# Modulation passes of a two-layer encoder trunk: pinned to other places in four stages, with their buffers kept to the end and 2 KB of scratch for dynamic transfers

## The chip, the cores and the metric

The kernel runs on one core of one Trainium2 chip. The metric is the time of one execution on the device in microseconds (us); the runs shown are of the kernel before, three times, and one execution that was taken with the hardware profiler. TensorE is called PE, VectorE DVE, ScalarE ACT, GpSimd POOL, and SP is the engine whose queue issues nearly all transfers here.

## The reference, cut to what matters

One sequence of 512 tokens with 1024 features goes through two layers. Every norm is followed by a shift and a scale, and every residual add by a gate, and these vectors come from one conditioning vector `c`. The modulation is what the change is about:

```python
c_act = jax.nn.silu(c)
mod = c_act @ mod_w[layer] + mod_b[layer]                  # two layers, 6 vectors of 1024 each
sh1, sc1, g1, sh2, sc2, g2 = jnp.split(mod, N_MOD, axis=-1)
u = modulate(rms_norm(h, norm_mix[layer]), sh1, sc1)       # x * (1 + scale) + shift
mix = hgrn2_mixer(u, ...)  # layer 0;  chunk_band_attention(u, k_pad, v_pad, ...)  in layer 1
h = h + g1 * mix
u = modulate(rms_norm(h, norm_ffn[layer]), sh2, sc2)
h = h + g2 * swiglu(u, ffn_w_in[layer], ffn_w_out[layer])
# after layer 0 a shared K/V of the same h, with its own shift and scale (shk, sck)
```

So there are 14 modulation vectors, each 1024 long, each the product of a 1024 x 1024 matrix with one vector.

## The kernel before, in words

**Layout and stages.** The residual stream `h` lies in SBUF as 8 tiles of 128 features x 512 tokens. All weights stream from HBM in blocks of 512 KB, in the order of `weight_plan`, each split by ACT (line 123 or 496) and DVE (line 128 or 497) into a high and a low part, so that a product is three matmuls (lines 183 to 185). The stages in order of time are: start and first projections; the mixer of layer 0 (`core`, lines 712 to 852, four pairs of heads, whose DVE steps at lines 732 and 733 each must end before PE's next small products at line 757); its output projection `ao`; the first FFN; shared K/V and attention (lines 1109 to 1291); the second FFN.

**An FFN** (`ffn`, `fast_tiles`) has four plain hidden tiles, then 18 tiles of a Strassen-like scheme with 7 half-size products each (lines 531 to 533), for which DVE builds sums of weight blocks (`f_x`, lines 510 to 515) and their low parts (`f_w_l`, line 497), and then the output projection `f_o` in chunks. Both FFNs run the same code; only the first of them carries modulation work in the kernel before.

**A modulation pass.** A vector is computed on DVE, not on PE: for each of its 8 blocks of 128 outputs a row block of the matrix (128 x 1024, 512 KB, tile `mw`) is loaded by SP at line 313, and one DVE instruction at line 315 multiplies it with `crow` (the activated `c` in every partition) and adds up along the row; a second, short instruction (`DVE_READ_ACCUMULATOR`) writes the sum out. Eight passes make one vector (line 317). The first two vectors are done at the start in another way; the other twelve are 96 passes. Two buffers of tag `mraw` hold the rows, so a load waits until the pass before the last has been read.

**What sets the order.** `mod_vectors` is a Python generator, `side`; each `next(side)` emits one load and one pass. Before, six vectors were emitted in the mixer and the `ao` stage (48 passes: in `push` from position 50 of the filler on, at every 7th and later every 3rd position; then in `ao`, with the rest at n = 5), and six in the first FFN (48 passes: after every second fast tile, and after the output chunks). The emitted program then goes through a list scheduler that puts each engine's instructions in an order by a model of its own. `tc.issue_after(state["mods_after"].ins)` keeps a pass from standing ahead of the named instruction; in the kernel before, `mods_after` is set once near the start of the mixer (line 1028) and once for each input of a fast FFN (line 352), so that the scheduler is free to place the passes anywhere after those. Each engine executes its own order strictly, and SP issues its loads strictly in order, weights and `mw` rows in one queue.

**Memory.** The buffers of the passes (`mods`: `crow` and two `mraw`) are closed after the first FFN (line 1103). 16 KB of every partition are the default scratch for transfers that POOL issues; there are four of these (line 126), two in each FFN.

## Time and profile before

| what | value |
|---|---|
| median of 3 runs | 1267.31 us (1263.37 to 1268.36) |
| the profiled execution's own time | 1264.94 us |
| its span in the profile | 1263.2 us |
| granted TensorE clock, mean | 0.995 |
| PE busy | 1238.8 us (98%) |
| DVE busy | 986.2 us (78%) |
| ACT busy | 644.6 us (51%) |
| passes: busy time of line 315 | 116.8 us in 96, mean 1220 ns |

Shares of the page are averages over stages; the views by stretch (windows) give busy time of each engine between two moments. PE's matmuls are pipelined, so that a busy PE need not be at its peak; equal work that takes longer in one stage than in another shows the difference.

### The profile page before, as it was taken

The numbers are of one execution on the slowest core, as the hardware profiler recorded it, in microseconds if no ns is written. First come the engines' busy times: TensorE is split into PE (matmuls) and PEld (weight loads), VectorE is DVE, ScalarE is ACT, GpSimd is POOL, SyncE is SP. The second block draws the span as 40 slices with busy tenths as digits, with TensorE's granted clock in tenths as the row PEclk, the third lists the DMA queues.
The fourth block names the chain that finished last, engine by engine and source line by source line (L and its number), as shares of the span: only waits on it lengthen the run. The fifth ranks groups of instructions, "written<-read, shape, count | busy, mean of one in ns | idle before, by whom it ended". The sixth has DMA issues, their size and how long they took to land.

```text
span 1263.2 us, 21610 instructions
## 1 busy us (share of the span) xinstructions
PE 1238.8 (98%) x8560; PEld 1072.5 (85%) x8560; DVE 986.2 (78%) x1805; ACT 644.6 (51%) x1132; POOL 21.9 (2%) x29
## 2 busy tenths in 40 slices
PE   7999999999999999999999999999999999999997
PEld 6888778788899999978888877777889999998887
DVE  7998988947899999987357867776798888884323
ACT  4464446353645555653227656675465556574221
POOL 0000000000000000000000000000000000000000
PEclk8999999999999999999999999999999999999999
DMA  9455666613265555567333332221342332342331
GB/s 362 178 184 185 219 232 218 201 67 101 78 223 175 190 185 185 186 215 244 93 101 110 109 94 87 74 68 35 115 117 92 111 116 102 101 126 92 92 92 67
DMA packets 52533, 177.55 MB, mean 141 GB/s; under 512 B 5968, under 2 KB 8400, under 8 KB 52432
## 3 DMA queue, kind: packets, MB, share of 16 engines
q1 hardware_dynamic: 51856, 174.08, 41.2%
q0 software_dynamic: 576, 2.10, 1.0%
q8 instruction: 67, 1.10, 0.4%
q14 instruction: 34, 0.28, 0.1%
HBM read 171.96 MB, written 2.10 MB: 138 GB/s over the span
## 4 chain that ended last, share of the span: by engine, by line
PE 74%; DVE 12%; DMA 6%; ACT 4%; issue 3%; POOL 1%; SPq 0%; DVEq 0%; POOLq 0%; ACTq 0%
PE f_r L532 8%; PE f_r L533 7%; PE f_r L531 7%; PE f_o L185 6%; PE f_o L183 6%; PE f_o L184 6%; DVE mw L315 3%; DMA mw<-in_modw 2%; DMA r_f_c<-in_ffn_in 2%; DVE f_w_l L497 1%; PE ao L183 1%; PE ao L185 1%; PE ao L184 1%; PE av L206 1%; PE bo L183 1%
## 5 line engine op out<-in xcount | busy, mean ns | idle before, releaser
L532 PE MATMUL f_r<-f_l,f_w_h 128*128 128x256 f32 x1008 | 286.8, 285 | 0.0
L533 PE MATMUL f_r<-f_h,f_w_l 128*128 128x256 f32 x1008 | 282.1, 280 | 1.8 <-DVE f_w_l L497 1.7
L531 PE MATMUL f_r<-f_h,f_w_h 128*128 128x256 f32 x1008 | 280.8, 279 | 0.0
L533 PEld LDWEIGHTS f_r<-f_h,f_w_l 128*128 128x128 f32 x1008 | 189.0, 188 | 3.2 <-DVE f_w_l L497 3.0
L531 PEld LDWEIGHTS f_r<-f_h,f_w_h 128*128 128x128 f32 x1008 | 189.5, 188 | 0.3 <-ACT f_pu L553 0.2
L532 PEld LDWEIGHTS f_r<-f_l,f_w_h 128*128 128x128 f32 x1008 | 189.5, 188 | 0.1
L183 PE MATMUL f_o<-f_p,f_o_h 128*128 128x512 f32 (+1 forms) x374 | 142.3, 380 | 0.0
L184 PE MATMUL f_o<-f_p,f_o_h 128*128 128x512 f32 (+1 forms) x374 | 140.9, 377 | 1.0 <-DVE f_p L448 1.0
L185 PE MATMUL f_o<-f_p,f_o_l 128*128 128x512 f32 (+1 forms) x374 | 141.5, 380 | 0.2
L315 DVE SCALAR_TENSOR_TENSOR mw<-mw,crow 128x1024 f32<-128x1024 f32 x96 | 116.8, 1220 | 14.9 <-DMA mw<-in_modw 14.7
L123 ACT ACTIVATE f_o_h<-r_f_o 128x1024 fp32r<-128x1024 f32 (+1 forms) x48 | 46.8, 987 | 135.0 <-PE f_o L184 100.6
L128 DVE TENSOR_TENSOR f_o_l<-r_f_o,f_o_h 128x1024 fp32r<-128x1024 f32 (+1 forms) x48 | 54.0, 1133 | 70.6 <-ACT f_o_h L123 64.2
L496 ACT ACTIVATE f_w_h<-f_x 128x1024 fp32r<-128x1024 f32 x72 | 76.5, 1062 | 48.8 <-PE f_r L532 41.4
L497 DVE TENSOR_TENSOR f_w_l<-f_x,f_w_h 128x1024 fp32r<-128x1024 f32 x72 | 88.0, 1223 | 5.0 <-ACT f_w_h L496 2.6
L496 ACT ACTIVATE f_w_h<-r_f_c 128x1024 fp32r<-128x1024 f32 x72 | 61.0, 847 | 49.2 <-PE f_r L532 48.4
L185 PEld LDWEIGHTS f_o<-f_p,f_o_l 128*128 128x128 f32 x374 | 70.1, 188 | 16.0 <-DVE f_o_l L128 1.9
L184 PEld LDWEIGHTS f_o<-f_p,f_o_h 128*128 128x128 f32 x374 | 70.2, 188 | 15.1 <-DVE f_p L448 1.4
L183 PEld LDWEIGHTS f_o<-f_p,f_o_h 128*128 128x128 f32 x374 | 70.3, 188 | 12.5
L497 DVE TENSOR_TENSOR f_w_l<-r_f_c,f_w_h 128x1024 fp32r<-128x1024 f32 x72 | 68.8, 955 | 10.0 <-ACT f_w_h L496 10.0
L1179 ACT ACTIVATE sb<-sb,st 128x128 f32<-128x128 f32 (+1 forms) x64 | 35.7, 558 | 36.4 <-DVE st L1178 36.1
L1176 DVE CUSTOM_DVE_ANT_0 sb<-s,wb 128x128 f32<-128x128 f32 (+1 forms) x64 | 30.8, 486 | 15.0 <-PE s L1173 14.8
L185 PE MATMUL f<-f_h,f_l 128*128 128x512 f32 x96 | 37.4, 396 | 0.0
(397 smaller groups left out, 2728.1 us busy)
## 6 DMA issues: line engine op xcount, KB each, us to landing
mw<-in_modw SPq DMA_DIRECT2D x96, 512.0 KB, 4.2
r_f_c<-in_ffn_in SPq DMA_DIRECT2D x72, 512.0 KB, 3.4
r_f_o<-in_ffn_out SPq DMA_DIRECT2D x32, 512.0 KB, 3.6
mrow<-in_modw SPq DMA_DIRECT2D x16, 512.0 KB, 8.8
r_f<-in_ffn_in SPq DMA_DIRECT2D x16, 512.0 KB, 3.4
r_f_o<-in_ffn_out SPq DMA_DIRECT2D x16, 384.0 KB, 3.2
r_av<-in_a_v SPq DMA_DIRECT2D x8, 512.0 KB, 3.9
r_g<-in_a_g SPq DMA_DIRECT2D x8, 512.0 KB, 4.7
```

The costliest lines, as they stand in the source:

```text
L123: A.activation(wh, raw, AF.Copy)
L128: V.tensor_sub(wl, raw, wh)
L183: T.matmul(ps, wh[:, kt, :], uh, start=start, stop=False)
L184: T.matmul(ps, wh[:, kt, :], ul, start=False, stop=False)
L185: T.matmul(ps, wl[:, kt, :], uh, start=False, stop=stop)
L315: V.scalar_tensor_tensor(mw, mw, 1.0, crow, op0=ALU.mult, op1=ALU.mult, accum_out=raw[:, j:j + 1])
L496: A.activation(wh, raw, AF.Copy)
L497: V.tensor_sub(wl, raw, wh)
L531: T.matmul(ps, wh[:, j, :], uh, start=f, stop=False, skip_group_check=True)
L532: T.matmul(ps, wh[:, j, :], ul, start=False, stop=False, skip_group_check=True)
L533: T.matmul(ps, wl[:, j, :], uh, start=False, stop=stop and j == 3, skip_group_check=True)
L1179: A.activation(s[:, 0:n], s[:, 0:n], AF.Exp, bias=st[:, 1:2], accum_out=st[:, 2:3])
```

## The change

**How passes are emitted.** `mod_vectors` becomes one generator over all steps of the vectors that it is given. It loads its rows ahead: one row ahead with the two `mraw` buffers, or two rows ahead when it is given a second pool, in which two more buffers (`mraw2`) hold every other row. Its first `next` only loads.

**Where.** 32 passes (g1, sc2, sh2, g2) in the mixer, at every 5th position of the filler from 55 on, with four buffers, and none in `ao`; 40 in the first FFN (sck, shk, sc1b, sh1b, g1b), after two of three fast tiles, two after each chunk of the first output pair and four for each later output tile, with four buffers; 16 in attention (sc2b, sh2b), at every third unit of scores, two buffers; 8 in the second FFN (g2b), after two of three fast tiles.

**Pinned.** `mods_after` now follows the program: it is set by the low splits of the mixer's and the output projections' weights, by the second instruction of `advance` in the mixer, by the last instruction of each fast tile and by the normalising multiply of each unit of scores. A pass cannot stand earlier than the latest of these at the moment when it was emitted.

**Memory.** The scratch for POOL's transfers is 2 KB, and the `mods` pool stays open to the end of the kernel.

```diff
-            V.tensor_sub(wl, raw, wh)
+            low = V.tensor_sub(wl, raw, wh)
+            if key[0] in ("av", "g", "zf", "q", "ao") or key[1] == "o":
+                state["mods_after"] = low
...
+    def mod_vectors(names, extra=None):
+        steps = [(vectors.index(v), j) for v in names for j in range(KT)]
+        ahead = 2 if extra else 1
...
+                pool, tag = (extra, "mraw2") if extra and n % 2 else (mp, "mraw")
+                rows[n] = pool.tile([P, D], F32, tag=tag, name=f"mw{i}_{j}", bufs=2)
+                nc.sync.dma_start(out=rows[n], in_=d["modw"][i, j])
...
+        for n, (i, j) in enumerate(steps):
+            load_row(n + ahead)
...
             with tc.issue_after(state["mods_after"].ins):
                 V.scalar_tensor_tensor(mw, mw, 1.0, crow, op0=ALU.mult, op1=ALU.mult, accum_out=raw[:, j:j + 1])
...
-                    for _ in range(3):
+                    for _ in range(2):
                         next(side, None)
...
-                        for _ in range(1 + (fast and ci < 2)):
+                        for _ in range(1 + (fast and ci == 0)):
                             next(side, None)
...
-            V.tensor_mul(row2, row2, p5)
+            last = V.tensor_mul(row2, row2, p5)
             kept(n, at)
-            if i % 2:
+            if i % 3:
+                state["mods_after"] = last
                 next(side, None)
...
-            V.tensor_mul(kv, kv, t2[:, :, 1:2].to_broadcast([P, n, hh]))
+            state["mods_after"] = V.tensor_mul(kv, kv, t2[:, :, 1:2].to_broadcast([P, n, hh]))
...
-    side = mod_vectors(("g1", "sc2", "sh2", "g2", "sck", "shk"))
+    side = mod_vectors(("g1", "sc2", "sh2", "g2"), hp)
+    MODS_FROM = 55
...
-            if pos > 49 and pos % (7 if pos < 114 else 3) == 0:
+            if pos >= MODS_FROM and pos % 5 == 0:
                 next(side, None)
...
-    side = mod_vectors(("sc1b", "sh1b", "g1b", "sc2b", "sh2b", "g2b"))
...
-    ffn(0, z0, u, mod["g2"], side, finish)
-    mods.close()
+    with tc.tile_pool(name="mx", bufs=1) as mx:
+        ffn(0, z0, u, mod["g2"], mod_vectors(("sck", "shk", "sc1b", "sh1b", "g1b"), mx), finish)
...
-            V.tensor_scalar_mul(s[:, 0:n], s[:, 0:n], st[:, 3:4])
+            state["mods_after"] = V.tensor_scalar_mul(s[:, 0:n], s[:, 0:n], st[:, 3:4])
...
+        side = mod_vectors(("sc2b", "sh2b"))
...
+            if k % 3 == 2:
+                next(side, None)
...
-    ffn(1, z0, u, mod["g2b"], iter(()), finish)
+    ffn(1, z0, u, mod["g2b"], mod_vectors(("g2b",)), finish)
...
-    nc = _bacc.Bacc("TRN2", target_bir_lowering=False, num_devices=1)
+    nc = _bacc.Bacc("TRN2", target_bir_lowering=False, num_devices=1, dynamic_dma_scratch_size=2048)
```

**How it moves instructions.** Three places on DVE. The passes are the rows with `mw`; their line is 315 before and 334 in the changed kernel, and other lines are shifted likewise.

The first place is the mixer, at the start of the second pair of heads; `zf_l` and `q_l` are low parts of weights, and `qq` and `ks` the steps that PE's next small products wait for. Before:

```order
L315 SCALAR_TENSOR_TENSOR mw_4_1798,mcol_1673<-mw_4_1798,crow 128x1024
L128 TENSOR_TENSOR q_l<-r_q_1284,q_h 128x1024
L315 SCALAR_TENSOR_TENSOR mw_5_1829,mcol_1673<-mw_5_1829,crow 128x1024
L315 SCALAR_TENSOR_TENSOR mw_6_1841,mcol_1673<-mw_6_1841,crow 128x1024
L128 TENSOR_TENSOR zf_l<-r_zf_1374,zf_h 128x1024
L732 TENSOR_TENSOR qq_508<-qq_508,f_509 128x512
L733 TENSOR_TENSOR ks_906<-ks_906,f_509 128x512
```

The same place in the changed kernel:

```order
L861 TENSOR_TENSOR oe_1270<-o_1233,ors_1254 128x512
L127 TENSOR_TENSOR q_l<-r_q_1291,q_h 128x1024
L127 TENSOR_TENSOR zf_l<-r_zf_1384,zf_h 128x1024
L752 TENSOR_TENSOR qq_508<-qq_508,f_509 128x512
L753 TENSOR_TENSOR ks_906<-ks_906,f_509 128x512
```

The passes ahead of `zf_l`, `qq` and `ks` are gone from here; the next one stands six rows further down.

The second place is the first FFN, between the steps of its fast tiles 8 and 9 (`f_w_l` are the low parts that PE waits for). Before:

```order
L497 TENSOR_TENSOR f_8_w_l<-r_f_8_c_4005,f_8_w_h 128x512
L515 TENSOR_TENSOR f_9_x_4263<-r_f_9_c_4129,f_9_x_4262 128x512
L560 TENSOR_TENSOR f_pu_4195<-f_r_8_4194,f_pu_4195 128x256
L315 SCALAR_TENSOR_TENSOR mw_2_6058,mcol_5961<-mw_2_6058,crow 128x1024
L497 TENSOR_TENSOR f_9_w_l<-r_f_9_c_4129,f_9_w_h 128x1024
L567 TENSOR_TENSOR f_ar_3936<-f_qu_4196 128x256
L568 TENSOR_TENSOR f_ar_3936<-f_r_8_4193,f_pu_4195 128x256
L315 SCALAR_TENSOR_TENSOR mw_3_6061,mcol_5961<-mw_3_6061,crow 128x1024
L497 TENSOR_TENSOR f_9_w_l<-f_9_x_4262,f_9_w_h 128x1024
```

The same place in the changed kernel:

```order
L518 TENSOR_TENSOR f_8_w_l<-r_f_8_c_3956,f_8_w_h 128x512
L581 TENSOR_TENSOR f_pu_4147<-f_r_8_4146,f_pu_4147 128x256
L518 TENSOR_TENSOR f_9_w_l<-r_f_9_c_4084,f_9_w_h 128x1024
L588 TENSOR_TENSOR f_ar_3887<-f_qu_4148 128x256
L589 TENSOR_TENSOR f_ar_3887<-f_r_8_4145,f_pu_4147 128x256
L590 TENSOR_TENSOR f_ar_3887<-f_ar_3887,f_pu_4147 128x256
L518 TENSOR_TENSOR f_9_w_l<-f_9_x_4214,f_9_w_h 128x1024
L518 TENSOR_TENSOR f_9_w_l<-f_9_x_4215,f_9_w_h 128x1024
L593 TENSOR_TENSOR f_ar_3887<-f_ar_3887,f_qu_4148 128x256
L334 SCALAR_TENSOR_TENSOR mw_1_3885,mcol_4016<-mw_1_3885,crow 128x1024
```

One pass is left for this tile, and it stands behind the low parts shown; among the rows of the fast tiles as a whole ten passes are left.

The third place is attention, at the seventh pair of heads: `sb` is a unit of scores, `ta` and `tb` the query parts that PE's next scores wait for, `bo_l` a low part of a later weight. Before:

```order
L1178 TENSOR_SCALAR st_3_8612<-st_3_8612 128x1
L1180 RECIPROCAL st_3_8612<-st_3_8612 128x1
L1181 TENSOR_SCALAR sb_3_8611<-sb_3_8611,st_3_8612 128x512
L1155 SCALAR_TENSOR_TENSOR ta_8628<-bq_8558,ta_8628 64x512
L1156 SCALAR_TENSOR_TENSOR tb_8629<-bq_8558,tb_8629 64x512
L128 TENSOR_TENSOR bo_l<-r_bo_8634,bo_h 128x1024
```

The same place in the changed kernel:

```order
L1195 TENSOR_SCALAR st_3_8584<-st_3_8584 128x1
L127 TENSOR_TENSOR bo_l<-r_bo_8609,bo_h 128x1024
L1197 RECIPROCAL st_3_8584<-st_3_8584 128x1
L1198 TENSOR_SCALAR sb_3_8583<-sb_3_8583,st_3_8584 128x512
L334 SCALAR_TENSOR_TENSOR mw_6_8509,mcol_8117<-mw_6_8509,crow 128x1024
L1172 SCALAR_TENSOR_TENSOR ta_8603<-bq_8530,ta_8603 64x512
L1173 SCALAR_TENSOR_TENSOR tb_8604<-bq_8530,tb_8604 64x512
```

Both the weight's low part and a pass now stand ahead of `ta`. The fourth pair's `ta` is preceded in the same way; at the other pairs no pass stands directly ahead of it.

More of the change, by code (lines that the diff above doesn't have):

```diff
@@ L1 @@
 from contextlib import ExitStack
-from itertools import chain as _chain
 import numpy as np
@@ L306, in modulated, with load_row @@
         return uh, ul
-    def mod_vector(i, bcol, mc):
-        raw = sm.tile([P, KT], F32, tag="mcol", name=f"mcol{i}", bufs=2)
-        for j in range(KT):
-            mw = mp.tile([P, D], F32, tag="mraw", name=f"mw{i}_{j}", bufs=2)
-            nc.sync.dma_start(mw, d["modw"][i, j])
+    def mod_vectors(names, extra=None):
+        steps = [(vectors.index(v), j) for v in names for j in range(KT)]
+        ahead = 2 if extra else 1
+        rows, raw = {}, None
+        def load_row(n):
+            if n < len(steps):
+                i, j = steps[n]
+                pool, tag = (extra, "mraw2") if extra and n % 2 else (mp, "mraw")
+                rows[n] = pool.tile([P, D], F32, tag=tag, name=f"mw{i}_{j}", bufs=2)
+                nc.sync.dma_start(out=rows[n], in_=d["modw"][i, j])
+        for n in range(ahead):
+            load_row(n)
+        yield
+        for n, (i, j) in enumerate(steps):
+            load_row(n + ahead)
+            if j == 0:
+                raw = sm.tile([P, KT], F32, tag="mcol", name=f"mcol{i}", bufs=2)
+            mw = rows.pop(n)
             with tc.issue_after(state["mods_after"].ins):
                 V.scalar_tensor_tensor(mw, mw, 1.0, crow, op0=ALU.mult, op1=ALU.mult, accum_out=raw[:, j:j + 1])
+            if j == KT - 1:
+                bcol = C_MB + 8 * i
+                V.tensor_add(mod[vectors[i]], raw, cols[:, bcol:bcol + KT])
             yield
-        V.tensor_add(mc, raw, cols[:, bcol:bcol + KT])
     def drain(gen):
@@ L571, in fast_tiles @@
             A.activation(p5, r1, AF.Silu)
-            V.tensor_mul(row2, row2, p5)
+            last = V.tensor_mul(row2, row2, p5)
             kept(n, at)
-            if i % 2:
+            if i % 3:
+                state["mods_after"] = last
                 next(side, None)
+        state["mods_after"] = last
         fetch(state["used"] - 1, 1)
@@ L667, in trunk @@
     mod = {v: cst.tile([P, KT], F32, tag=f"mod_{v}", name=f"mod_{v}") for v in vectors[2:]}
-    def mod_vectors(names):
-        return _chain.from_iterable(mod_vector(vectors.index(v), C_MB + 8 * vectors.index(v), mod[v]) for v in names)
     def gates(p, zs):
@@ L1050, in trunk @@
         ysplit(hd)
+    drain(side)
     part = []
@@ L1071, in trunk @@
             res = []
-            for i, _ in enumerate(proj(("ao", n), y, res)):
-                if i % 3 == 2:
-                    next(side, None)
+            drain(proj(("ao", n), y, res))
             ps = res[0]
-        if n == 5:
-            drain(side)
         residual(n, ps, mod["g1"])
@@ L1270, in trunk @@
         drain(fill)
+        drain(side)
         acc = sm.tile([P, S], F32, tag="nacc", name="acc3", bufs=1)
```

## The prediction

> **What bounds the kernel now.** I read the page's engine table first, for the engine that is busy all the time:
>
> ```profile
> PE 1238.8 (98%) x8560; PEld 1072.5 (85%) x8560; DVE 986.2 (78%) x1805; ACT 644.6 (51%) x1132; POOL 21.9 (2%) x29
> ```
>
> PE is the bound: it is idle for 1263.2 - 1238.8 = 24.4 us of the whole span. The change gives PE no less work, so all that it can win is time in which PE stands or runs below its pace because DVE is late. Next I read the busy times by stretch, cut at the stages, to find where that is:
>
> ```profile
> core 0: us, PE busy (x) PEld busy (x) DVE busy (x) ACT busy (x) POOL busy (x), PEclk, DMA share, GB/s
> 20.00:72.00 52.00, 51.96 (x219) 42.24 (x219) 51.09 (x84) 21.61 (x32) 2.06 (x1) 0.96 0.61 226
> 125.00:175.00 50.00, 47.29 (x576) 38.39 (x576) 43.40 (x79) 25.33 (x51) 1.95 (x2) 1.00 0.65 212
> 175.00:222.00 47.00, 46.30 (x567) 37.83 (x566) 42.90 (x76) 23.99 (x49) 1.99 (x2) 1.00 0.68 224
> 222.00:265.00 43.00, 41.27 (x545) 33.08 (x544) 32.83 (x55) 17.62 (x41) 1.64 (x1) 1.00 0.49 160
> 357.00:541.00 184.00, 182.20 (x1515) 180.47 (x1514) 181.51 (x300) 106.73 (x183) 0.00 (x0) 1.00 0.57 190
> 541.00:567.00 26.00, 24.77 (x107) 19.40 (x106) 22.84 (x39) 13.47 (x22) 0.00 (x0) 1.00 0.57 202
> 567.00:668.00 101.00, 101.00 (x446) 82.93 (x444) 55.26 (x82) 29.00 (x35) 0.40 (x4) 1.00 0.47 151
> 700.00:885.00 185.00, 182.48 (x949) 142.18 (x949) 137.76 (x428) 115.71 (x252) 0.00 (x0) 1.00 0.24 78
> 951.00:1131.00 180.00, 180.00 (x1514) 179.91 (x1513) 155.24 (x233) 106.09 (x183) 0.00 (x0) 1.00 0.32 106
> ```
>
> The first row is the first projections, with PE never idle. The next three are the mixer from its second pair of heads on: PE idle 2.71 + 0.70 + 1.73 = 5.1 us. Then come the fast tiles of the first FFN: DVE is full (181.5 of 184). The last row is the same stage of the second FFN, which has no passes: DVE has air, and PE stands nowhere. Between them are the start of the first FFN's output projection, 1.2 us idle, its rest, where DVE is half empty, and attention, 2.5 us idle. The first and last products of the fast tiles give the two stages' lengths exactly:
>
> ```profile
> L531 PE MATMUL f_r<-f_h,f_w_h x504: 276/279/382, 356.7 to 540.1; 128*128 128x256 f32 x168
> ...
> L531 PE MATMUL f_r<-f_h,f_w_h x504: 278/279/280, 951.4 to 1130.8; 128*128 128x256 f32 x168
> ```
>
> 183.4 us against 179.4: the same 1512 matmuls take 4.0 us longer beside the passes. So the whole of what can be won is about 5.1 + 4.0 + 1.2 = 10.3 us.
>
> By the Trainium skill (Perfetto Trace Analysis, section Identifying the Most-Contended Engine) matmul busy time is a poor measure of headroom and weight-load busy time a better one; matmul idle time alone would set this stage's term at 1.8 us (184 - 182.20), weight-load idle at 3.5 (184 - 180.47). The trace agrees with the rule: the two lengths differ by 4.0. My term is from the lengths.
>
> **The change part by part.** What a pass costs and where the passes are:
>
> ```profile
> L315 DVE SCALAR_TENSOR_TENSOR mw<-mw,crow x48: 1215/1220/1227, 74.9 to 244.4; 128x1024 f32<-128x1024 f32 x48
> ...
> L315 DVE SCALAR_TENSOR_TENSOR mw<-mw,crow x34: 1208/1219/1228, 344.9 to 540.0; 128x1024 f32<-128x1024 f32 x34
> ...
> 125.00:175.00 50.00, 19.56 (x32) 1.00 0.65 212
> ```
>
> The last row is line 315 alone in one stretch: 32 instructions are 16 passes, so a pass with its short second instruction takes 19.56 / 16 = 1.22 us of DVE. 48 passes lie in the mixer, 34 about the fast tiles, the other 14 in the output projection.
>
> *Mixer, 48 to 32 passes.* It frees 16 x 1.22 = 19.5 us of DVE. What PE gets of it is bounded by its idle 5.1 us. The chain of waits, the longest pieces at the second pair of heads, shows how one idle piece came about:
>
> ```profile
> 126.20 1.24 DVE mw L315 x3
> 127.46 4.43 DMA mw<-in_modw
> ...
> 133.21 1.14 DVE zf_l L128
> 134.35 0.60 DVE qq L732
> 134.96 0.61 DVE ks L733
> ...
> 135.70 0.75 PE fine L757 x48
> ```
>
> A pass must end before its buffer is loaded again; the load takes 4.4 us; the pass that needs it stands in DVE's order ahead of `zf_l`, `qq` and `ks`; and PE waits for `ks`. In the changed order those passes are not there (first of the three places above), and rows come two ahead into four buffers, so that the wait for a row should go. PE's waits in the mixer, DVE's for rows there, and those of SP's queue for a buffer of a row:
>
> ```profile
> PE fine L757 <- DVE ks L733: 2.6, 5, 0.7
> PE ot L850 <- DVE oe L841: 1.1, 1, 1.1
> ...
> DVE mw L315 <- DMA mw<-in_modw: 6.2, 8, 1.5
> ...
> SPq L313 <- DVE mw L315: 80.7, 38, 4.5
> ```
>
> The 1.1 us before `ot` follow POOL's power and stay in part. What is late next is `zf_l`, `g_l` and the remaining passes, which still stand between steps of the later pairs. I take 3.0 us (the waits on `ks` and a little more); bounds 0 and 5.1. The loads that are moved all sit in SP's queue among the weights. SP stood 80.7 us there until a pass had freed a row's buffer, with weights queued behind; with four buffers it stands less. Two rows now come early, ahead of loads of the first projections; PE is not idle there (51.96 of 52), so I take nothing, and bound it by the waiting time of one load, 1 to 2 us.
>
> *First FFN, fast tiles, 34 to 10 passes.* DVE goes from 181.5 to about 181.5 - 24 x 1.22 = 152 us of the stage, less than the second FFN's 155, with which PE kept its pace. Ten passes are left, each behind a tile's last step. If the 4.0 us scale with the passes, 24/34 of them go, 2.8; if a DVE with air costs nothing, 4.0. I take 3.4.
>
> *First FFN, output projection.* Here 14 passes become 30. The idle 1.2 us at its start come from `f_p` behind passes and `f_o_l`; fewer passes stand ahead of the first sums now, and I take 0.8 (bounds 0 and 1.2). In the rest, 55 of 101 us of DVE and at most 22 more passes, 27 us, leave a fifth of it free: nothing, at most 2 us lost where the last passes stand among the weighted sums for the next norm, with the next pair of weights queued behind them on DVE.
>
> *Attention, 0 to 16 passes.* 19.5 us of DVE work are added to a stage where DVE is busy 138 of 185. The trace before shows no pass here, so I bound it. How DVE stands at a pair of heads:
>
> ```profile
> 792.81 0.16 DVE L1180 RECIPROCAL st<-st 128x1 f32<-128x1 f32 x1 [0.94 <-ACT sb L1179]
> ...
> 793.90 0.68 DVE L1155 SCALAR_TENSOR_TENSOR ta<-bq,ta 64x512 fp32r<-64x512 f32 x1 [0.40 <-ACT tb L1154]
> ...
> 795.34 1.23 DVE L128 TENSOR_TENSOR k_l<-r_k,k_h 128x1024 fp32r<-128x1024 f32 x1
> ...
> 794.64 0.33 PE L1172 MATMUL s<-ka,ta 128*128 128x128 f32 x1 [0.42 <-DVE ta L1155]
> ```
>
> DVE waits 0.94 and 0.40 us for ACT ahead of `ta`, and PE's scores wait for `ta`. Where the weight's low part (1.23) and a pass (1.22) both move ahead of `ta`, it comes 1.23 + 1.22 - 0.94 - 0.40 = 1.1 us later; this is so at two pairs (third place above): 2.2 us. At the other pairs the low part alone fits into the two waits. The other 14 passes stand in the chain of scores, behind whose waiting instructions DVE's later scores queue; DVE's own waits there are the cover:
>
> ```profile
> DVE st L1180 <- ACT sb L1179: 17.0, 27, 0.9
> DVE sb L1176 <- PE s L1173: 14.8, 15, 3.5
> ```
>
> 31.8 us, more than the passes need, and the scores run three units ahead of their transposes. I take 2.2; the lower bound is 0, the upper is every pass in full, 19.5 us; below nothing is excluded, since a stage that only gets work added cannot gain by it.
>
> *Second FFN, 0 to 8 passes.* 155 + 9.8 = 165 of 180 us, still below the first FFN's 181.5. At the first FFN's rate (4.0 / 34 a pass) it would be 0.9; with DVE below full I take 0.3.
>
> *Scratch and buffers kept.* POOL's four transfers run in 2 KB in place of 16. I take nothing (rival three).
>
> Sum: -3.0 - 3.4 - 0.8 + 2.2 + 0.3 = -4.7 us, against the profiled execution's own 1264.94 (span 1263.2 and 1.7 around it): 1260.2. The median of the three runs is 2.4 us above that execution; the four executions together have a mean of 1266.0. From there: 1261.3, forecast 1261, 0.4% below.
>
> **The rivals.**
>
> *One: everything that can be won is won.* PE's waits in the mixer and the first FFN all go and attention hides its passes: -10.3 + 0.3 = -10 us, 1256. For it: DVE gets air in each of the stages in which PE waits, and 31.8 us of waits in attention are there to be filled. Against it: `oe` behind POOL, the passes left in the mixer, and the passes right ahead of `ta`.
>
> *Two: the wait comes back in attention, slower than before.* If the passes delay scores and PSUM banks come free later, PE waits in each of the 16 places. From 0.83 us a pass on (7.2 us of gains less 0.3, plus 6.3, which are 0.5%, over 16) the kernel is slower by over 0.5%; with the full 1.22 it is +19.5 - 7.2 + 0.3 = +12.6, 1279. For it: attention is a chain through PE, DVE and ACT. Against it: DVE's waits there, and that the fuller DVE of the first FFN's tiles cost PE only 0.12 us a pass.
>
> *Three: the smaller scratch holds POOL's transfers up.* The two transfers of an FFN, as POOL issues them:
>
> ```profile
> 341.00 1.05 POOL L126 DMA_DIRECT2D f_l<-r_f  x1 [24.63 <-DVE f_s L362]
> 344.48 0.86 POOL L126 DMA_DIRECT2D f_l<-r_f  x1 [2.44 <-ACT f_l L125]
> ...
> f_l<-r_f POOLq DMA_DIRECT2D x4, 512.0 KB, 5.0
> ```
>
> If the second had to wait until the first has landed (5.0 us), it would start 5.0 - 3.5 = 1.5 us later, in two FFNs 3 us in all if nothing hid it: 1264. Beside it, the Trainium skill (SBUF — State Buffer, section SBUF size: 192, 224, or 256?) says that this scratch is the ring of descriptors of POOL's transfers; no run here shows how full it gets. Two transfers are in flight at most.
>
> *Four: PE's waits move rather than go.* The first FFN's 4.0 us may come from weights that land late behind `mw` rows, and with four buffers and the same bytes they would still. Then the mixer gives 1 us, the tiles 1, attention takes 2: 1266, no change. Against it: the second FFN, with the same weights on the same queue, loses nothing.
>
> **How the numbers follow.** Chances: forecast 0.52, rival one 0.27, four 0.12, two 0.06, three 0.03. A measurement of this kernel can tell about 0.5%, 6.3 us, from no change; as a difference between like runs my sum of -4.7 lies 1.6 us short of that limit. Of the forecast's chance I give a quarter to faster (0.13), and 0.25 of rival one's: 0.38. Slower is rival two and no other: 0.06. The rest, 0.56, is no change. The range: down to rival one's 1256 less a little for how executions differ, 1255; up past rival four's 1266 to 8 us lost in attention half offset by a good mixer, 1268.
>
> **What would show it.** Right: the products of the first FFN's fast tiles span less than 181 us, PE is idle under 3 us from 125 us on in the mixer, no DVE wait on `mw` rows is left there, and attention is 1 to 4 us longer than 185 with PE waiting on `ta` at the fourth and the seventh pair. Wrong: fast tiles that still need 183 us (then the passes were not what slowed them); an attention longer by over 8 us; or a first FFN's output projection that PE waits in.

## The result and the profile after

| kernel | median, us | runs (lowest to highest) | profiled span, us |
|---|---|---|---|
| before | 1267.1 | 4 (1263.37 to 1268.36) | 1263.2 |
| changed | 1255.17 | 4 (1254.58 to 1255.99) | 1253.6 |

The ratio is 0.9913 (95% interval 0.99 to 0.9926): the change gains 0.9%. The forecast was 1261 with a range from 1255 to 1268, so the result lies 0.2 us inside the range's lower end, where rival one (all that can be won is won, 1256) had been put. The engine table of the changed kernel, to set beside the one of before:

```profile
PE 1235.1 (99%) x8560; PEld 1071.7 (85%) x8560; DVE 988.5 (79%) x1805; ACT 643.7 (51%) x1132; POOL 21.9 (2%) x29
```

PE's idle time went from 24.4 to 1253.6 - 1235.1 = 18.5 us, 5.9 of the 9.6 us by which the spans differ; the other 3.7 are less busy time for the same products. DVE's work did not shrink: it was moved. Busy times by stretch, cut in each kernel at the first product of a stage; first the mixer of before, from the first `fine` to the first `ao`:

```profile
86.60:265.90 179.30, 174.16 (x2222) 141.74 (x2221) 151.90 (x271) 83.08 (x178) 7.52 (x7) 1.00 0.60 197
```

And the changed kernel: the mixer, the first FFN's fast tiles, the start and the rest of its output projection, attention's scores, the second FFN's fast tiles (columns as in the prediction: PE, PEld, DVE, ACT, POOL, clock, DMA share, GB/s):

```profile
86.10:262.30 176.20, 173.88 (x2222) 141.81 (x2221) 137.35 (x236) 82.85 (x178) 7.50 (x7) 1.00 0.48 154
...
353.10:532.90 179.80, 179.80 (x1514) 179.78 (x1513) 164.28 (x255) 106.29 (x183) 0.00 (x0) 1.00 0.42 134
532.00:558.00 26.00, 25.89 (x117) 20.78 (x116) 23.89 (x37) 14.63 (x24) 0.00 (x0) 1.00 0.65 195
558.00:659.00 101.00, 101.00 (x446) 82.97 (x445) 71.11 (x115) 29.00 (x35) 0.40 (x4) 1.00 0.70 227
700.50:855.70 155.20, 153.51 (x814) 120.13 (x814) 131.88 (x430) 99.88 (x228) 0.00 (x0) 1.00 0.43 135
941.60:1121.60 180.00, 180.00 (x1514) 179.93 (x1513) 162.26 (x250) 106.25 (x183) 0.00 (x0) 1.00 0.39 123
```

In the mixer PE's idle time fell from 5.1 to 2.3 us. The fast tiles have lost theirs altogether, with DVE at 164 in place of full; the output projection starts with 0.1 us of idle in place of 1.2; and attention with 16 passes is no longer than without them. Its row of before, cut at the same products:

```profile
709.50:865.50 156.00, 153.61 (x816) 120.44 (x816) 116.15 (x394) 99.80 (x228) 0.00 (x0) 1.00 0.25 81
```

The first and last products of the fast tiles, which span 179.4 us now in the first FFN, as they do in the second:

```profile
L552 PE MATMUL f_r<-f_h,f_w_h x504: 278/279/280, 353.1 to 532.5; 128*128 128x256 f32 x168
```

PE's waits for `ta` in attention before and in the changed kernel, and DVE's waits in attention as a whole in the changed kernel, those that the prediction had named as cover:

```profile
PE s L1172 <- DVE ta L1155: 1.8, 4, 0.6
...
PE s L1189 <- DVE ta L1172: 0.7, 2, 0.4
...
DVE st L1197 <- ACT sb L1196: 10.6, 16, 1.0
DVE sb L1193 <- PE s L1190: 5.4, 6, 2.7
```

DVE's 31.8 us of waits are 16.0 now, so they did take the passes' work up; PE waited 1.8 us for `ta` before and waits 0.7 now.

Stage by stage, as the time between the first starts of the named products on PE in the two profiled executions:

| stage | before | changed | difference | forecast |
|---|---|---|---|---|
| start to the first `fine` | 86.6 | 86.1 | -0.5 | 0 |
| mixer (first `fine` to first `ao`) | 179.3 | 176.2 | -3.1 | -3.0 |
| `ao` and plain tiles | 90.9 | 90.9 | 0.0 | 0 |
| first FFN, fast tiles | 183.7 | 179.8 | -3.9 | -3.4 |
| first FFN, output projection | 122.9 | 121.4 | -1.5 | -0.8 |
| shared K/V to the first scores | 46.2 | 46.2 | 0.0 | 0 |
| attention's scores, first to last | 156.0 | 155.2 | -0.8 | +2.2 |
| its output and plain tiles | 85.9 | 86.2 | +0.3 | 0 |
| second FFN, from its fast tiles to the last product | 305.0 | 305.0 | 0.0 | +0.3 |
| sum | | | -9.5 | -4.7 |

The sum has missed by 4.8 us, and 3.0 of these are attention's. The start differs from execution to execution (85.1 to 88.2 us over the profiles of this study, whatever the kernel) and isn't the change's. The stages of before differ too. Its mixer took 179.3, 180.9, 180.2 and 181.6 us in the four profiles with that mixer, a mean of 180.5 (180.1 without the last, which has a granted clock of 0.99 there); the changed mixer has 175.6 to 176.4 in seven, a mean of 176.0. So the mixer's part is 4.0 to 4.5 rather than 3.1 us. The fast tiles of before took 182.4 us, not 183.7, in the profile of the run with the small scratch, so their part is 2.6 to 3.9. The medians differ by 11.9 us, but three later sets of 13 to 25 runs of the kernel before have medians of 1265.5 to 1265.9, and against these the gain is 10.4 to 10.7.

### The profile page after: what moved, and what is told of

Same layout as the page of the kernel before. It is cut to its first block, busy times and chain, and to the rows that moved or that the text cites. A ratio compares the mean times of both kernels' runs of the same rounds, so it can differ in the third digit from the quotient of the medians.

```text
span 1253.6 us, 21593 instructions
## 1 busy us (share of the span) xinstructions
PE 1235.1 (99%) x8560; PEld 1071.7 (85%) x8560; DVE 988.5 (79%) x1805; ACT 643.7 (51%) x1132; POOL 21.9 (2%) x29
## 4 chain that ended last, share of the span: by engine, by line
PE 84%; DVE 8%; ACT 3%; DMA 2%; issue 2%; SPq 0%; DVEq 0%; POOLq 0%; ACTq 0%
PE f_r L553 10%; PE f_r L554 9%; PE f_r L552 9%; PE f_o L186 6%; PE f_o L185 6%; PE f_o L184 6%; PE f L184 2%; PE f L185 2%; PE f L186 2%; PE o L847 1%; PE g L184 1%; PE g L185 1%; PE bo L184 1%; PE bo L186 1%; PE ao L186 1%
## 5 line engine op out<-in xcount | busy, mean ns | idle before, releaser
L185 PE MATMUL f<-f_l,f_h 128*128 128x512 f32 x96 | 37.2, 394 | 0.0
```

The source lines that it names most:

```text
L185: T.matmul(ps, wh[:, kt, :], ul, start=False, stop=False)
```

## The experiments

Theory at this point: PE lost time where DVE had too much to do for PE's pace (fast tiles) or a pass too near a step that PE waits for (mixer), and attention had room for 16 passes. Rivals: the smaller scratch or the buffers matter; rows held the weights up; the pins alone did it; attention has room for any number.

**The scratch alone.** In the kernel before:

```
-    nc = _bacc.Bacc("TRN2", target_bir_lowering=False, num_devices=1)
+    nc = _bacc.Bacc("TRN2", target_bir_lowering=False, num_devices=1, dynamic_dma_scratch_size=2048)
```

> The kernel before, with nothing changed but the scratch for POOL's transfers, 2 KB for 16. Theory (the scratch does nothing; all of the gain is in where the passes stand): 1264 to 1268 us, each stage within 0.5 us of the kernel before, and the second of POOL's two transfers in an FFN issued within 4 us of the first. Rival three of the prediction: the second transfer is held until the first has landed, 1.5 us an FFN, 1267 to 1270 us.

Measured: 1265.93 us, ratio to before 0.9997 (0.9986 to 1.0008). Nothing. POOL's two transfers of the first FFN stand as far apart as they did:

```profile
341.08 1.05 POOL L126 DMA_DIRECT2D f_l<-r_f  x1 [24.59 <-DVE f_s L362]
344.57 0.87 POOL L126 DMA_DIRECT2D f_l<-r_f  x1 [2.45 <-ACT f_l L125]
```

3.49 us between them, 3.48 before. Rival three is out. The Trainium skill (SBUF — State Buffer, section SBUF size: 192, 224, or 256?) calls this scratch a ring of descriptors; at two transfers of 512 KB in flight 2 KB of it cost nothing here.

**Without the pins.** In the changed kernel, all the new settings of `mods_after` are taken out, for example:

```
-                state["mods_after"] = last
                 next(side, None)
```

> The changed kernel without its pins: the same emission, buffers and scratch, but a pass may stand anywhere behind the instruction that the kernel before named. The scheduler then puts all 16 passes of attention and 30 in all between the low parts of the first FFN's fast tiles, and passes ahead of the second pair's zf_l in the mixer again. Theory (the pins do it, by keeping DVE's work in the fast tiles below its limit): fast tiles of the first FFN 182 to 184 us in place of 179.4, mixer 1 to 3 us longer than in the changed kernel, 1259 to 1262 us in all. Rival (rows loaded further ahead into four buffers do it): 1255 to 1257 us, fast tiles 179.4.

Measured: 1262.65 us, ratio to before 0.9967 (0.9954 to 0.998). The scheduler moves passes up, attention's into the first FFN and its output projection's into the fast tiles:

```profile
354.60:537.90 183.30, 182.40 (x1513) 180.51 (x1512) 181.59 (x301) 106.56 (x183) 0.00 (x0) 1.00 0.59 193
...
354.60:537.90 183.30, 37.71 (x63) 1.00 0.59 193
...
86.30:263.90 177.60, 174.49 (x2222) 142.69 (x2221) 134.49 (x236) 82.74 (x178) 7.48 (x7) 0.99 0.43 146
```

The second row is the passes alone: 63 instructions, 31 or 32 passes, and the stage is back at 183.3 us with DVE full. The third is the mixer: 177.6 us, 1.6 more than pinned, although only 28 of its 32 passes start in it, the others ahead of it. But the granted clock was 0.83 from 140 to 150 us there, which is worth up to 1.7 us (an estimate, 0.17 of 10 us), so what the pins do for the mixer isn't settled by this run. In the fast tiles it is: the emission alone leaves the stage as it was, and the pins keep the passes where they were meant to go.

**35 passes in the fast tiles, pinned.** In the changed kernel:

```
-            if i % 3:
+            for _ in range(2 if nm == "f0" else i % 3 > 0):
                 state["mods_after"] = last
                 next(side, None)
```

> The changed kernel with two passes after every fast tile of the first FFN, pinned behind the tile's last instruction as before: 35 passes in the fast tiles in place of 10, and five left for the output projection. Theory A (it is the amount of DVE work in the stage that slows it): 25 more passes of 1.14 to 1.22 us on 163.9 busy us are 192 to 194 us of DVE, more than the 179.4 that PE needs, so the fast tiles take 186 to 194 us and the kernel 1262 to 1270. Theory B (it is that passes stand directly ahead of low parts that PE waits for): pinned behind a tile's last step they cost little, fast tiles 179.4 to 181, kernel 1255 to 1257.

Measured: 1264.45 us, ratio to before 0.9991 (0.9981 to 1.0001).

```profile
352.20:537.60 185.40, 183.76 (x1513) 181.04 (x1512) 182.64 (x301) 103.60 (x183) 0.00 (x0) 1.00 0.59 195
...
352.20:537.60 185.40, 39.14 (x66) 1.00 0.59 195
...
PE f_o L185 <- DVE f_p L469: 2.5, 1, 2.5
```

33 passes, all behind a tile's last step, and the stage is 5.6 us longer, with 2.5 us of waiting behind it when the output projection needs DVE's first sums. Theory B fails: the pin behind a tile's last step does not make this many passes cheap. Theory A fits in kind, and overrated the size (186 to 194 expected). But the run does not part the amount of DVE work from its place. A pass behind one tile's last step can still stand ahead of the next tile's low parts: in DVE's order 11 of the 33 stand directly ahead of a low part and 16 more with one pass between (directly, 21 of 31 before and none of the ten in the changed kernel). In the changed kernel both the number and the place are better, and which of them counts for more in the fast tiles stays open. By the Trainium skill (Perfetto Trace Analysis, section Identifying the Most-Contended Engine) weight-load busy time measures PE's slack better than matmul busy time; here the weight loads are idle for 4.4 us and the matmuls for 1.6, so the rule points the right way, and still falls short of the 5.6 us that the lengths show.

**48 passes in the mixer, pinned, four buffers.** In the changed kernel:

```
-    side = mod_vectors(("g1", "sc2", "sh2", "g2"), hp)
+    side = mod_vectors(("g1", "sc2", "sh2", "g2", "sck", "shk"), hp)
...
-            if pos >= MODS_FROM and pos % 5 == 0:
+            if pos >= MODS_FROM and pos % 10 in (0, 3, 6):
```

and `sck` and `shk` leave the first FFN's list.

> The changed kernel with the mixer given 48 passes as in the kernel before (sck and shk come back into it, at three of ten positions), still pinned and with four buffers; the first FFN then has 24 passes in place of 40. Theory A (the mixer's 3 us came from fewer passes): most of it is lost, 1257 to 1259 us, PE idle in the mixer 4 to 5 us. Theory B (it came from the pin and from rows that are there in time): PE idle stays at 2 to 3 us and the kernel at 1255 to 1256.5.

Measured: 1258.11 us, ratio to before 0.9936 (0.992 to 0.9953).

```profile
85.90:264.70 178.80, 174.22 (x2222) 141.63 (x2221) 155.25 (x271) 83.08 (x178) 8.33 (x7) 1.00 0.61 198
```

PE is idle 4.6 us again. Against the changed kernel's mean of 176.0 the 16 passes cost 2.8 us, 0.17 a pass, as theory A has it. That is not yet their part in the gain, for the kernel before has only 44 of its 48 passes in this stretch (90 instructions; the other four run ahead of the first `fine`):

```profile
86.60:265.90 179.30, 53.83 (x90) 1.00 0.60 197
```

So the change takes 12 passes out of the stretch, at 0.17 each 2.1 of the 4.0 to 4.5 us (an estimate). The rest, 1.9 to 2.4, is left for the order that emission and pins make: each is about half. In the expectation's words, theory A has the kernel's time right (1257 to 1259) and theory B a share of the cause.

**Two buffers, one row ahead.** In the changed kernel:

```
-    side = mod_vectors(("g1", "sc2", "sh2", "g2"), hp)
+    side = mod_vectors(("g1", "sc2", "sh2", "g2"))
...
-        ffn(0, z0, u, mod["g2"], mod_vectors(("sck", "shk", "sc1b", "sh1b", "g1b"), mx), finish)
+        ffn(0, z0, u, mod["g2"], mod_vectors(("sck", "shk", "sc1b", "sh1b", "g1b")), finish)
```

> The changed kernel with two buffers for rows and one row ahead in the mixer and the first FFN, as in the kernel before; counts and pins stay. Theory (amount and place of DVE's work do it, rows are never late): within 0.5 us of the changed kernel, 1255 to 1256. Rival (the four buffers do the mixer's part): DVE waits for rows in the mixer as in the kernel before (6.2 us there), mixer 1 to 3 us longer, 1256 to 1258.

Measured: 1254.99 us, ratio to before 0.9911 (0.9897 to 0.9926), the same as the changed kernel. DVE does wait for rows again, and PE doesn't feel it:

```profile
DVE mw L334 <- DMA mw<-in_modw: 6.1, 3, 3.5
...
87.00:262.90 175.90, 174.35 (x2222) 141.68 (x2221) 137.41 (x236) 82.91 (x178) 7.60 (x7) 1.00 0.50 160
```

So 6.1 us of waiting for rows cost nothing in this order, and the four buffers do nothing here. Nor does PE's loss need such a wait: with 48 passes and four buffers DVE waited 1.1 us for a row in the mixer, and PE was idle for 4.6. What the wait did in the order of before no run shows by itself.

**Rows without passes, passes without rows.** In the kernel before, in the first FFN alone:

```
+            nn = P if state.get("short") else D
...
-                V.scalar_tensor_tensor(mw, mw, 1.0, crow, op0=ALU.mult, op1=ALU.mult, accum_out=raw[:, j:j + 1])
+                V.scalar_tensor_tensor(mw[:, 0:nn], mw[:, 0:nn], 1.0, crow[:, 0:nn], op0=ALU.mult, op1=ALU.mult, accum_out=raw[:, j:j + 1])
```

> The kernel before, with the first FFN's 48 rows still loaded, but each pass cut to 128 of its 1024 columns (six vectors are sums over an eighth of their terms). DVE is relieved, the transfers are not. Theory (DVE's full queue slows the fast tiles): they take 179.4 to 180 us in place of 183.4, their output projection starts without its 1.2 us of idle, 1260 to 1262 us. Rival four of the prediction (weights land late behind rows in SP's queue): fast tiles 183 us, 1265 to 1266 us.

```
-            mw = mp.tile([P, D], F32, tag="mraw", name=f"mw{i}_{j}", bufs=2)
-            nc.sync.dma_start(mw, d["modw"][i, j])
+            if "row" in state:
+                mw, junk = state["row"]
...
-                V.scalar_tensor_tensor(mw, mw, 1.0, crow, op0=ALU.mult, op1=ALU.mult, accum_out=raw[:, j:j + 1])
+                V.scalar_tensor_tensor(junk, mw, 1.0, crow, op0=ALU.mult, op1=ALU.mult, accum_out=raw[:, j:j + 1])
```

> The kernel before with the first FFN's 48 passes in full, but all on one row that is loaded once, the product written to another buffer (six vectors are not computed): DVE's work stays, 24 MB of transfers go. Theory (DVE): fast tiles 183 to 184 us, 1264 to 1267 us. Rival four (weights behind rows): fast tiles 179.4 us, 1260 to 1262 us.

Measured: passes without rows 1264.43 us, ratio 0.9991 (0.9981 to 1.0); rows without passes 1275.18 us, ratio 1.0071 (1.0056 to 1.0086). The fast tiles with passes and no rows:

```profile
359.00:541.00 182.00, 181.39 (x1514) 180.25 (x1513) 181.18 (x300) 106.74 (x183) 0.00 (x0) 1.00 0.33 104
```

And with rows and cut passes, with the waits of DVE and SP and the cut passes' own row:

```profile
356.60:552.00 195.40, 186.32 (x1514) 182.55 (x1513) 162.37 (x330) 106.44 (x183) 0.00 (x0) 0.99 0.63 213
...
DVE mw L316 <- DMA mw<-in_modw: 10.8, 17, 2.0
DVE f_x L511 <- DMA r_f_c<-in_ffn_in: 9.6, 6, 2.2
...
SPq L313 <- DMA mw<-in_modw: 60.3, 24, 6.1
...
357.00:552.00 195.00, 12.51 (x87) 0.99 0.63 212
```

Without any row the stage still takes 182.0 us, so 2.2 of the excess over 179.8 are DVE's work alone. With the rows of before it was 183.7 in one profile and 182.4 in the run with the small scratch, so that the rows' own share lies between 0.4 and 1.7 us and is not settled. The other run doesn't measure what it was made for: the cut passes were packed closer, probably because the scheduler counts them as short: 87 instructions or 43 passes into the stage where before had 31 (the last section has its row). DVE waits 10.8 us for rows and 9.6 for weights from the same queue, so in this run the loads and not the passes hold the stage up. It does show that rival four's mechanism exists, at more rows than either kernel has there.

**No passes in attention.** In the changed kernel:

```
-        side = mod_vectors(("sc2b", "sh2b"))
+        side = iter(())
+        V.tensor_copy(mod["sc2b"], mod["sc1b"])
+        V.tensor_copy(mod["sh2b"], mod["sh1b"])
```

> The changed kernel without attention's 16 passes and their rows: the second FFN's shift and scale are copies of attention's, so two of the 14 vectors are not computed. The scheduler's order on PE and DVE in attention is then that of the kernel before. The prediction's term (a pass and a low part ahead of ta at two pairs cost 2.2 us): attention 2.2 us shorter than in the changed kernel, 1253 us. What the two traces say (the changed kernel's attention is 0.3 us shorter than before): 1255 to 1256 us.

Measured: 1256.74 us, ratio to before 0.9929 (0.9915 to 0.9944): no faster than with them (the sums of `sc2b` and `sh2b` are left out; 2.1 us of its profiled span is a longer start). The scores take 156.0 us, as before, 0.8 more than with the passes:

```profile
702.30:858.30 156.00, 153.63 (x816) 120.50 (x816) 116.11 (x394) 99.83 (x228) 0.00 (x0) 1.00 0.26 81
```

**Attention's passes twice and three times.** In the changed kernel, with `more` 1 or 2 for attention alone:

```
+                for _ in range(more):
+                    V.scalar_tensor_tensor(mw, mw, 1.0, crow, op0=ALU.mult, op1=ALU.mult, accum_out=spare[:, j:j + 1])
```

> The changed kernel with every pass of attention done twice, one behind the other on the same row (the second sum goes to a spare column and is not used): 32 passes of DVE time, the same 16 rows. Theory (DVE's own waits for ACT and PE are the cover, and the scheduler sets weight products ahead of scores that come late): DVE goes from 153.9 to about 172 of 185 us and PE loses 0 to 3 us, 1255 to 1258. Rival (each pass delays the chain of scores, and only the first 16 fitted): 16 x 1.2 us, 1270 to 1275.

> The same with every pass of attention done three times, 48 passes of DVE time. By the theory that only DVE's free time counts, DVE needs about 154 + 32 x 1.15 = 191 us for a stage that PE does in 185: it becomes the bound, attention is 6 to 15 us longer, 1261 to 1270. If DVE's recorded waits were not the limit, 1255 to 1260.

Measured: 1270.0 us, ratio 1.0034 (1.0022 to 1.0046), and 1289.37 us, ratio 1.0187 (1.0172 to 1.0202). The scores with 32 passes:

```profile
702.50:868.30 165.80, 156.71 (x813) 120.29 (x813) 148.50 (x462) 100.02 (x227) 0.00 (x0) 0.99 0.40 127
...
PE t L1210 <- DVE sb L1201: 4.6, 6, 1.8
```

And with 48:

```profile
703.50:887.30 183.80, 162.10 (x812) 121.94 (x812) 166.02 (x494) 100.53 (x227) 0.00 (x0) 0.95 0.36 114
```

The first 16 cost nothing, the next 16 take 10.6 us, and 16 more 18.0, 1.1 each. My theory failed: DVE still stands idle for 17 us of each, so it is not DVE's free time that decides. The scores come late, and PE waits at the transposes (`t`); rival two's mechanism, PE paying for each pass, begins behind the sixteenth. Two things are mixed into these sizes. Some of the 10.6 us may be another effect of the spare column, see the last section; the 18.0 are free of it. And the granted clock was 0.99 and then 0.95 over the scores (0.91 from 780 to 800 us of the last run, 0.83 to 820, 0.86 from 840 to 860), where it was 1.00 with 16 passes. PE's busy time for the same products grew by 3.2 and then by 5.4 us, its standing by 7.4 and then by 12.6. So of the 1.1 us a pass 0.8 is standing; why the clock fell is not shown, for in the next run PE stands for 11.0 us of its scores at 1.00.

**PE's order held.** In the changed kernel, for the K projection's blocks from the fourth on, with `at` the first product of the scores of the pair before:

```
+                    at = state.get("scored", {}).get(2 * p - 2) if kt > 2 else None
...
+                        with tc.issue_after(at.ins):
+                            mm3(pk, wk, kt, ukv[kt], kt == 0, kt == KT - 1)
```

> The changed kernel with one more rule on PE's order: from the fourth block on, a K projection's products may not stand ahead of the first scores of the pair before. The scheduler had set 26 weight products ahead of the scores at the fourth and the seventh pair in the changed kernel, where the kernel before has 16; now there are 15 at each pair, and the passes still stand ahead of ta at those two pairs, the weight's low part behind it. Theory (the products moved ahead are what covers the late ta): PE waits for ta at the pairs again, 0.5 to 0.8 us at each of six, attention 1 to 4 us longer than in the changed kernel, 1256 to 1259. Rival (DVE's waits alone cover the passes): attention as in the changed kernel within 0.5 us, 1255.

Measured: 1265.89 us, ratio to before 1.0007 (0.9997 to 1.0018): the whole gain is lost. The same passes, and PE waits for `ta`:

```profile
699.50:864.10 164.60, 153.64 (x816) 120.57 (x816) 134.66 (x430) 100.69 (x228) 0.00 (x0) 1.00 0.40 128
...
PE s L1196 <- DVE ta L1179: 10.4, 5, 2.6
```

So the passes do make `ta` late, by more than I had counted; in the changed kernel PE has something else to do in that time. The hold is tighter than the order of before, though. It leaves nine products of the K projection between the last `bq` and the scores of the third to the seventh pair, where the kernel before has 15 at the third and ten at the others, and at 0.23 us a product that is some 2.3 of the 9.4 us by which the scores are longer (an estimate). The hold without the passes wasn't run. DVE and ACT at the sixth pair of this kernel show how `ta` comes late:

```profile
804.87 1.22 DVE L334 SCALAR_TENSOR_TENSOR mw<-mw,crow 128x1024 f32<-128x1024 f32 x1
...
806.01 0.69 DVE L1200 CUSTOM_DVE_ANT_0 sb<-s,wb 128x512 f32<-128x512 f32 x1
...
807.07 0.72 ACT L1203 ACTIVATE sb<-sb,st 128x512 f32<-128x512 f32 x1 [0.29 <-DVE st L1202]
...
807.79 0.57 ACT L1177 ACTIVATE ta<-bq 64x512 fp32r<-64x512 f32 x1
```

The pass stands ahead of a unit's maximum (`sb<-s,wb`), that unit's exponential stands in ACT's queue ahead of ACT's half of `ta`, and DVE's half, at 809.00, has waited 0.30 us for ACT. A pass need not stand right ahead of `ta` to delay it, so the waits come at five pairs and not at two.

**Going on.** In the changed kernel, 24 passes in the mixer, 40 in the first FFN and 24 in attention:

```
-    side = mod_vectors(("g1", "sc2", "sh2", "g2"), hp)
+    side = mod_vectors(("g1", "sc2", "sh2"), hp)
...
-            if pos >= MODS_FROM and pos % 5 == 0:
+            if pos >= MODS_FROM and pos % 7 == 0:
...
-        side = mod_vectors(("sc2b", "sh2b"))
+        side = mod_vectors(("g1b", "sc2b", "sh2b"))
...
-            if k % 3 == 2:
+            if k % 3:
```

with `g2` first in the first FFN's list in place of `g1b`.

> An attempt to go on: 24 passes in the mixer in place of 32 (g2 goes to the first FFN, which needs it at its end), 40 in the first FFN, 24 in attention (g1b in front, which its output projection needs) and 8 in the second FFN. From 48 passes to 32 the mixer went from 178.84 to 176.21 us, 0.16 us a pass; at that rate eight more give 1.3 us, and PE's idle time left in the mixer bounds it at 2.3. Attention's eight more cost 0 to 1 us if DVE's waits cover them. 1253.5 to 1255.5 us; if attention gives it back, 1255 to 1257.

Measured: 1259.33 us, ratio to before 0.9945 (0.9929 to 0.9962). The mixer and the scores:

```profile
85.30:259.40 174.10, 173.55 (x2221) 141.85 (x2221) 128.89 (x219) 82.69 (x178) 7.49 (x7) 1.00 0.41 131
...
697.50:859.40 161.90, 155.60 (x816) 120.86 (x816) 139.98 (x447) 98.87 (x227) 0.00 (x0) 0.99 0.50 156
```

The mixer gains 2.1 us and is idle for 0.6; attention gives 6.7 back for eight passes, 0.84 each (4.6 of it standing, the rest busy time at a granted clock of 0.99). By these rows a kernel with 24 passes in the mixer, 48 in the first FFN (whose output projection is half empty on DVE), 16 in attention and 8 in the second FFN would come to about 1253 us, an estimate (1255.17 less the mixer's 2.1); it wasn't run.

## Why the prediction was right or wrong, point by point

- **The time** came out inside the range, but by 0.2 us, and two of the four runs (1254.58 and 1254.98) lie below it. That is luck as much as insight: the sum had half of the change of the stages (-4.7 of -9.5). The prediction gave no change the largest chance, 0.56, and faster 0.38; the measured interval, 0.99 to 0.9926, is faster, clear of no change. Of the signs named for being right the first three came (fast tiles 179.4 us, PE idle for 2.3 us in the mixer, no wait of DVE for a row there), and the fourth, a longer attention, did not.
- **Where PE's time was lost** was right: mixer, fast tiles, and the output projection's start gave nearly all of the gain.
- **Mixer, -3.0.** -3.1 between the two profiles, -4.0 to -4.5 between the means of several. The size is near, the reason only half right. It was the order and the number of passes, about half each; a loss of PE's does not need the wait for a row that the prediction put at the head of the chain (the run with 48 passes). And the count was off: 12 passes leave the stretch, not 16.
- **Fast tiles, -3.4.** -3.9 between the two profiles, -2.6 against the other profile of before: all of the loss went, rival one's bound. Ten passes leave DVE at 164 of 180 us and cost nothing, 31 to 33 fill it and cost 2.2 to 5.6, so the loss isn't in proportion to the passes; whether it is DVE's fullness alone or also the passes' place isn't settled. The stage of before held 31 or 32 passes, not the 34 of the sum.
- **Output projection, -0.8 and 0.** -1.2 at its start, the whole idle time, and -0.3 in the rest, where DVE took 71 in place of 55 us and PE never stood.
- **Attention, +2.2: the step that failed.** It measured -0.8. It counted 1.1 us of delay of `ta` at two pairs against an order of PE that it took as given, and held a gain impossible, since the stage only got work added. The delay is real, and larger, but the list scheduler had answered it on the other engine. At the seventh pair PE's order before had ten products of the next pair's K projection between the last `bq` and the scores:

```profile
829.51 0.39 PE L185 MATMUL bq<-uqh,bq_l 128*128 128x512 f32 x1
829.73 0.39 PE L183 MATMUL k<-ukvh,k_h 128*128 128x512 f32 x1
...
831.79 0.39 PE L183 MATMUL k<-ukvh,k_h 128*128 128x512 f32 x1
832.60 0.33 PE L1172 MATMUL s<-ka,ta 128*128 128x128 f32 x1 [0.43 <-DVE ta L1155]
```

In the changed kernel there are twenty, 4.6 us of them (and ten again in the run without attention's passes), while DVE runs the low part and the pass:

```profile
820.73 0.39 PE L186 MATMUL bq<-uqh,bq_l 128*128 128x512 f32 x1
820.95 0.39 PE L184 MATMUL k<-ukvh,k_h 128*128 128x512 f32 x1
...
825.27 0.39 PE L185 MATMUL k<-ukvl,k_h 128*128 128x512 f32 x1
825.75 0.33 PE L1189 MATMUL s<-ka,ta 128*128 128x128 f32 x1
...
822.02 1.23 DVE L127 TENSOR_TENSOR bo_l<-r_bo,bo_h 128x1024 fp32r<-128x1024 f32 x1 [0.17 <-ACT bo_h L122]
...
823.76 1.22 DVE L334 SCALAR_TENSOR_TENSOR mw<-mw,crow 128x1024 f32<-128x1024 f32 x1
...
825.01 0.69 DVE L1172 SCALAR_TENSOR_TENSOR ta<-bq,ta 64x512 fp32r<-64x512 f32 x1
```

The scores start 4.8 us after the first of these products (825.75 - 820.95), 2.9 before (832.60 - 829.73): `ta` is 1.9 us later, more than the 1.1 of the sum, and PE works through it. The run with PE's order held puts a price on this: 9.4 us of the scores' length, some 2 of them from the hold itself. The prediction looked at the order of DVE there and not at that of PE.
- **Second FFN, +0.3.** 0.0: DVE 162 of 180 us, and PE never idle.
- **Scratch, 0.** Shown by itself.
- **The rivals.** Rival one was the outcome, but for the 2.3 us that PE still idles in the mixer. Rival two's price was near (1.1 us a pass beyond the 32nd, 0.7 to 0.8 from the 17th, with a lower granted clock in all of these), its point of onset was not: it had the first pass paid. Three is out. Four is out for this change; its mechanism appears at 43 rows in the stage.

## What to carry to other kernels

In this kernel side work on a busy helper engine was free up to a point in a stage and was paid beyond it, nearly in full in attention, at a fraction of its duration in the fast tiles. So weigh the amount in each stage, and its place, against the pace of the engine that bounds it; spread it until every stage is below that point, and look for the point by doubling the work. Where a scheduler sets the order, read what it did on the engine that waits as well as on the one that got the work: a delay may already have been filled. And a wait that the profile shows, as DVE's for rows here, is a cost only if something for the bound engine stands behind it.

## What the runs showed of the hardware that I had not expected

- **DVE's records overlap.** Instructions that stand back to back overlap by about 0.08 us in the trace (in the rows above a pass starts at 804.87 and takes 1.22, and the next but one starts at 806.01). So in a full stage the busy time is less than the sum of durations. The passes alone in the first FFN's fast tiles, before:

```profile
357.00:541.00 184.00, 37.85 (x63) 1.00 0.57 190
```

and in the changed kernel:

```profile
353.10:532.90 179.80, 12.26 (x20) 1.00 0.42 134
```

Outside them DVE shows 181.5 - 37.9 = 144 us before and 164.3 - 12.3 = 152 us now, for the same work: its durations add up to 165.5 us in both. I had reckoned with 152 in all after the change; it was 164. Some of that is the count of passes (21 or 22 left the stage, not 24), the rest is that work taken out of a full stage frees less busy time than its durations.
- **A small tile elsewhere changed PE's pace.** The kernels with repeated passes have one more tile, of 8 columns. In stages where nothing else differs, PE's products run otherwise, alike in both of these kernels; here `ao`, first the changed kernel:

```profile
L184 PE MATMUL ao<-yq,ao_h x32: 388/388/477, 262.3 to 304.3; 128*128 128x512 f32 x32
```

and the one with passes done twice:

```profile
L184 PE MATMUL ao<-yq,ao_h x32: 396/399/475, 261.9 to 304.7; 128*128 128x512 f32 x32
```

42.0 against 42.8 us. Two kernels without that tile that ran on the same chip (no passes in attention, PE's order held) take 90.7 us for `ao` and the plain tiles, these two 91.6. Over the whole kernel it is 4 to 5 us: the two output projections are longer by 2.1 to 2.2 each, the fast tiles 0.6 us each shorter. That the other tiles' places in memory shift is the likely cause; no run tried it.
